# First block of a seven-product matmul with GELU: half of its contraction by eight plain products, taken as the tiles arrive

## The chip, the core and the metric

The kernel runs on one core of one Trainium2 chip. The metric is the device time of one execution in microseconds (us); lower is better. The kernel before takes 1603.82 us, the median of three runs that lie between 1603.33 and 1605.74 us. A separate profiled execution took 1601.1 us.

## The reference

```python
def reference(a, b):                      # a, b: 4096 x 4096, float32
    x = np.matmul(a, b)
    return 0.5 * x * (1 + np.tanh(np.sqrt(2 / np.pi) * (x + 0.044715 * x**3)))
```

One product of two 4096 x 4096 matrices, and the tanh form of GELU on each element of the result.

## The kernel before, in words

**Seven products for eight.** A, B and the output are cut into quadrants of 2048 x 2048, named "11", "12", "21", "22". A plain product of 2 x 2 quadrants needs eight quadrant products. This kernel makes seven, of sums and differences of quadrants (the list `PRODUCTS`), and puts the output together from running sums of them. The inputs are converted to fp16 on their way in and the products are summed in fp32.

**Groups.** The output is made in 16 groups (`groups`, four row blocks by four column blocks). A group makes one 512 x 512 piece of each of the four output quadrants. For it, each product has 512 rows, 512 columns and half of the contraction, 2048. A product is done in four steps (`QPH`, counted by `q`), each a contraction of 512. A step is 16 matmuls of 128x128 weights by 512 columns: four row tiles `i` times four pieces `j`. A group is therefore 7 x 4 x 16 = 448 matmuls, and the kernel 7168.

**Tiles.** A block of a quadrant is loaded in two chunks `c` of 1024 of the contraction, so steps q = 0, 1 of a product read chunk 0 and steps 2, 3 read chunk 1. A chunk is 1 MB in fp16, of A or of B. The first group needs 16 of them: four quadrants of A and four of B, two chunks each. `load_a` (L126 to L136) issues four DMAs of 256 KB into a `stage` tile, of which there are two (`bufs=2`). `turn_a` (L138 to L144) transposes the stage on the vector engine (DVE) into `aT`. `load_b` (L146 to L156) issues eight DMAs of 128 KB, each to 32 partitions, and its tiles need no transpose. All these loads are issued by GpSimd (POOL), in the order in which the program calls them.

**Sums.** `make_sums` (L248 to L260) makes the sum or difference that a step multiplies, for A (`aS`), for B (`bS`) or for both, on DVE (L256). It is called two steps ahead (`AHEAD = 2`, three buffers each). An operand that is a single quadrant is used as it was loaded.

**Banks and settling.** A group has two sets of four PSUM banks, X and Y, one bank for each row tile. Each of the seven products adds to X or to Y. When a product ends (`q == 3`), `settle` (L321 to L351) takes what is needed from the banks, one row tile at a time: copies by the scalar engine (ACT) in `keep` (L297), additions and subtractions on DVE in `tt` (L319), GELU by ACT in `emit` (L310) and the write of an output tile by a DMA that SyncE (SP) issues (L313). Output tiles rotate through four buffers `y`. After the product s = 3, for example, ACT copies X, and DVE makes two operations for each row tile.

**What sets the order.** The whole program is written out by hand (`manual_schedule`). For each step, the loop at its end (L442 to L451) first issues what `before` lists for it (loads, transposes, and in later groups squares that serve a range check of the inputs), then the sums for two steps later, then output tiles that wait, then the matmuls with their settling. Each engine works through its own list in that order. For the first group the loads and transposes are listed in one table (L361 to L374): first A11 chunk 0, B12 and B22 chunk 0, then chunk 1 of the same three, and so on. The first product is A11 times (B12 + B22), so the first matmul needs those three tiles. The next group's B tiles are loaded from the products s = 3, 4 and 6 on (L384 to L407), into slots that are free by then (`move_slots`).

Of the kernel before, what the change touches and what calls it, by code (L numbers as in the profile page):

```python
# [7 lines left out]
F32 = mybir.dt.float32  # L8
F16 = mybir.dt.float16
BF16 = mybir.dt.bfloat16  # L10
# [3 lines left out]
ALU = mybir.AluOpType  # L14
AX = mybir.AxisListType

P = 128
Q = 32
NC = 512
# [3 lines left out]
RT = 4  # L23
TM = RT * P
AHEAD = 2
# [12 lines left out]
]  # L38
NP = len(PRODUCTS)
QPH = 4  # L40


SQUARE_MAX = 2.0**26
# [45 lines left out]
def half_path(  # L89
# [9 lines left out]
    nc = tc.nc  # L99
    M, K = a.shape  # L100
    _, N = b.shape
# [5 lines left out]
    pool = ctx.enter_context(tc.tile_pool(name="sb", bufs=1))  # L107
    psum_pool = ctx.enter_context(tc.tile_pool(name="psum", bufs=1, space=bass.MemoryType.PSUM))
# [12 lines left out]
    a_tiles, b_tiles = {}, {}  # L121
    a_slot = {"11": 0, "12": 1, "22": 2, "21": 3}
    b_slot = {"12": 0, "22": 1, "21": 2, "11": 3}
# [34 lines left out]
    def part(tiles, blk, quad, q):  # L158

        t = tiles[blk, quad, q // 2].rearrange("p x y -> p (x y)")  # L160
        w = 4 * NC
        return t[:, (q % 2) * w : (q % 2 + 1) * w]

    energy, squares = {}, []
    W = 2 * NC
# [82 lines left out]
    def make_sums(mb, nb, s, q):  # L248
        _, oa, ob = PRODUCTS[s]
        got = []  # L250
        for tiles, blk, o, tag in ((a_tiles, mb, oa, "aS"), (b_tiles, nb, ob, "bS")):
            if isinstance(o, str):
                got.append(part(tiles, blk, o, q))
                continue
            t = pool.tile([P, 4 * NC], F16, name=tag, tag=tag, bufs=AHEAD + 1)
            nc.vector.tensor_tensor(  # L256
                out=t[:, :], in0=part(tiles, blk, o[0], q), in1=part(tiles, blk, o[1], q),
                op=ALU.add if o[2] > 0 else ALU.subtract,
            )
            got.append(t)  # L260
        sums[mb, nb, s, q] = got

    groups = []
# [5 lines left out]
    banks = {}  # L269
    post = {}  # L270

    def multiply(gi, s, q):
        mb, nb = groups[gi]
        chain = PRODUCTS[s][0]
        first = q == 0 and (s == 0 or s == 1)
        sa, sb = sums.pop((mb, nb, s, q))
        sa = sa.rearrange("p (jj m e) -> p jj m e", jj=2, e=2)
        sb = sb.rearrange("p (kt n) -> p kt n", n=NC)
        for i in range(RT):
            if first:  # L280
                par = (gi + (chain == "Y")) % 2
                banks[chain, i] = psum_pool.tile([P, NC], F32, name=f"acc{chain}", tag=f"bank{par}{i}")
            for j in range(4):
                nc.tensor.matmul(  # L284
                    banks[chain, i][:, :],
                    sa[:, j // 2, i * P : (i + 1) * P, j % 2],
                    sb[:, j, :],
                    start=first and j == 0,
                    stop=q == QPH - 1 and j == 3,
                    skip_group_check=True,  # L290
                )
            if q == QPH - 1:
                settle(gi, s, i)

    def keep(tag, src, bufs):
        t = pool.tile([P, NC], F32, name=tag, tag=tag, bufs=bufs)
        nc.scalar.copy(out=t[:, :], in_=src[:, :])  # L297
        return t
# [3 lines left out]
    def flush():  # L302

        for args in waiting:
            emit(*args)
        waiting.clear()

    def emit(gi, i, ih, jh, y, src):
        mb, nb = groups[gi]
        nc.scalar.activation(y[:, :], src[:, :], ACT.Gelu_apprx_tanh)  # L310
        r0 = ih * MH + mb * TM + i * P
        c0 = jh * NH + nb * NC
        nc.sync.dma_start(out=out[r0 : r0 + P, c0 : c0 + NC], in_=y[:, :])  # L313

    def new_y():
        return pool.tile([P, NC], F32, name="y", tag="y", bufs=4)

    def tt(o, x, y, op):
        nc.vector.tensor_tensor(out=o[:, :], in0=x[:, :], in1=y[:, :], op=op)  # L319

    def settle(gi, s, i):  # L321

        X, Y = banks.get(("X", i)), banks.get(("Y", i))
        if s == 1:
            m5 = keep("m5", X, 2)
            flush()
            y = new_y()
            tt(y, Y, m5, ALU.subtract)
            waiting.append((gi, i, 0, 1, y, y))
        elif s == 2:  # L330
            post["x7", i] = keep("x7", X, RT)
        elif s == 3:
            x1 = post["x1", i] = keep("x1", X, RT)
            x7 = post["x7", i]
            tt(x7, x1, x7, ALU.subtract)
            tt(x1, Y, x1, ALU.subtract)
        elif s == 4:
            y = new_y()
            emit(gi, i, 0, 0, y, X)
            x1 = post["x1", i]  # L340
            tt(x1, X, x1, ALU.add)
        elif s == 5:
            y = new_y()
            tt(y, post.pop(("x1", i)), Y, ALU.subtract)
            flush()
            waiting.append((gi, i, 1, 0, y, y))
        elif s == 6:
            y = new_y()
            tt(y, Y, post.pop(("x7", i)), ALU.add)
            flush()  # L350
            waiting.append((gi, i, 1, 1, y, y))  # L351


    before = {}

    def at(gi, s, q, fn, *args):
        before.setdefault((gi * NP + s) * QPH + q, []).append((fn, args))


    T0 = -3  # L360
    for step, quads in (  # L361
        (-3, ("A11 0", "B12 0", "B22 0", "T11 0", "A11 1", "B12 1", "B22 1")),
        (0, ("T11 1", "A12 0", "A12 1")),
        (2, ("T12 0", "A22 0", "B21 0")),
        (4, ("T12 1", "A22 1", "B21 1", "B11 0")),
        (6, ("T22 0", "B11 1", "A21 0")),
        (8, ("T22 1", "A21 1")),
        (18, ("T21 0",)),
        (20, ("T21 1",)),
    ):  # L370
        for what in quads:
            fn = {"A": load_a, "B": load_b, "T": turn_a}[what[0]]
            at(0, 0, step, fn, 0, what[1:3], int(what[4]))


    nxt_b = {"12": "22", "22": "21", "21": "12", "11": "11"}
# [7 lines left out]
    for gi in range(len(groups) - 1):  # L384
        (mb, nb), (mb1, nb1) = groups[gi], groups[gi + 1]
        na, nbb = mb1 != mb, nb1 != nb
        if na:
            at(gi, 3, 0, move_slots, a_slot, nxt_a)
        if nbb:
            at(gi, 3, 0, move_slots, b_slot, nxt_b)  # L390
        for c in range(CH):
            if nbb:
                at(gi, 3, 2 * c + 1, load_b, nb1, "12", c)
                at(gi, 4, 2 * c + 1, load_b, nb1, "22", c)
                at(gi, 6, 2 * c + 1, load_b, nb1, "21", c)
            if na:
                at(gi, 4, c, load_a, mb1, "11", c)
                at(gi, 5, 2 * c, turn_a, mb1, "11", c)
                at(gi, 5, 2 * c + 1, load_a, mb1, "12", c)
                at(gi, 6, 2 * c, turn_a, mb1, "12", c)  # L400
                at(gi, 6, 2 * c + 1, load_a, mb1, "22", c)
                at(gi + 1, 0, 2 * c + 1, turn_a, mb1, "22", c)
                at(gi + 1, 1, c, load_a, mb1, "21", c)
                at(gi + 1, 3 + c, 0, turn_a, mb1, "21", c)
            if nbb:
                at(gi, 6, 2 * c + 1, load_b, nb1, "11", c)


    for mb in range(NMB):
        for which, gi in (("b", mb * NNB + 1), ("a", mb * NNB + 2)):  # L410
# [4 lines left out]
            ]  # L415
            n_two = len(pieces) - NP * QPH + 2
            for x, piece in enumerate(pieces):
                n = max(x // 2, x - n_two)
                at(gi, n // QPH, n % QPH, square, which, blk, *piece)
                at(gi, (n + 1) // QPH, (n + 1) % QPH, add_squares)  # L420
            at(gi, 6, 2, weigh, which)
# [16 lines left out]
    at(len(groups) - 1, 4, 0, read)  # L438

    with tc.manual_schedule():  # L440
        steps = [(gi, s, q) for gi in range(len(groups)) for s in range(NP) for q in range(QPH)]
        for n in range(T0, len(steps)):  # L442
            for fn, args in before.get(n, ()):
                fn(*args)
            if 0 <= n + AHEAD < len(steps):
                gi, s, q = steps[n + AHEAD]
                make_sums(*groups[gi], s, q)
            flush()
            if n >= 0:
                multiply(*steps[n])  # L450
        flush()  # L451
    return said["value"]

# [1 line left out]
def kernel(tc: tile.TileContext, a: bass.AP, b: bass.AP, out: bass.AP):  # L455
    stands = half_path(tc, a, b, out)
    with tc.If(stands == 0):
        general_path(tc, a, b, out)
# [30 lines left out]
```

## Time and profile before

| | us |
|---|---|
| median of 3 runs | 1603.82 |
| profiled execution, its time | 1601.1 |
| profiled execution, its span | 1599.4 |
| TensorE (PE) busy with matmuls | 1554.7 |
| DVE busy | 1243.0 |
| ACT busy | 517.6 |
| POOL busy | 530.8 |

The span runs from the first to the last recorded instruction; the 1.7 us between it and the execution's time lie around it. Busy time is a sum over an engine's instructions. Since neighbouring matmuls overlap, their mean duration (L284, some 380 ns) is longer than the distance between two starts. The page also cuts the span into 40 slices of 40 us; a digit is a busy share in tenths, and PEclk is the clock that TensorE was granted, in tenths of full speed. "aS<-aT" means that the instruction writes the tile aS and reads the tile aT. In a list of groups the last column is the time for which the engine sat idle just before them, and what ended it.

### The profile page before, as it was taken

To read this page: it belongs to the slowest core of one execution; us is meant where nothing else is said; L and a number is where in the kernel's file an instruction comes from. 1 tells how busy PE (TensorE), PEld (TensorE's weight loads), DVE (VectorE), ACT (ScalarE), POOL (GpSimd) and SP (SyncE) were. 2 spreads that over 40 slices of the span, in tenths; PEclk is the share of its full clock that TensorE was granted. 3 is DMA by queue.
4 is the path that set the end of the run, shared out by engine and by line. 5 is a ranking of instruction groups with operands and counts; after the bars stand their busy time and mean duration, and the time that the engine had idled before them with its cause. 6 is when DMAs were issued, how large, how long until landed. Compare 5 with 4: busy or idle time off the path is not lost. (4 is left out here: it accounts for less than half of the span.)

```text
span 1599.4 us, 19504 instructions
## 1 busy us (share of the span) xinstructions
PE 1554.7 (97%) x7168; PEld 702.9 (44%) x7168; DVE 1243.0 (78%) x1368; ACT 517.6 (32%) x706; POOL 530.8 (33%) x964
## 2 busy tenths in 40 slices
PE   2899999999999999999999999999999999999998
PEld 1344444444444444444444444444444444444443
DVE  2777888867977788886778788887687778888774
ACT  0114446412111644532112354542111144464111
POOL 6554341440323244332123414345021443414300
PEclk9999999999999999999999999999999999999999
DMA  9998674790967688488296847778477885747802
GB/s 179 198 201 158 105 147 99 129 207 29 196 100 144 138 132 158 86 154 156 56 181 106 174 82 137 151 117 182 81 127 137 132 158 101 149 94 132 157 27 81
DMA packets 224791, 211.12 MB, mean 132 GB/s; under 512 B 19888, under 2 KB 191920, under 8 KB 224688
## 3 DMA queue, kind: packets, MB, share of 16 engines
q0 software_dynamic: 187392, 142.67, 61.1%
q1 hardware_dynamic: 37296, 67.13, 11.6%
q8 instruction: 58, 0.95, 0.2%
q14 instruction: 45, 0.37, 0.1%
HBM read 285.22 MB, written 67.11 MB: 220 GB/s over the span
## 5 line engine op out<-in xcount | busy, mean ns | idle before, releaser
L284 PEld LDWEIGHTS <-aS 128*128 128x128 f16 x5120 | 501.4, 98 | 614.5 <-issue 9.1
L152 POOL DMA_DIRECT2D bR<-in_b_dram x832 | 448.6, 544 | 720.2 <-DVE bS L256 357.8
L256 DVE TENSOR_TENSOR aS<-aT 128x2048 f16<-128x2048 f16 x320 | 388.1, 1219 | 157.8 <-PE accX L284 121.9
L284 PE MATMUL accX<-bS,aS 128*128 128x512 f16 x2048 | 446.9, 380 | 8.6 <-DVE bS L256 7.4
L256 DVE TENSOR_TENSOR bS<-bR 128x2048 f16<-128x2048 f16 x320 | 387.7, 1218 | 80.2 <-PE accX L284 43.5
L284 PEld LDWEIGHTS <-aT 128*128 128x128 f16 x2048 | 201.5, 98 | 274.5 <-issue 23.1
L284 PE MATMUL accY<-bS,aT 128*128 128x512 f16 x1024 | 228.5, 385 | 29.1 <-DVE bS L256 29.1
L310 ACT ACTIVATE y<-y 128x512 f32<-128x512 f32 x192 | 118.6, 630 | 343.6 <-DVE y L319 343.3
L284 PE MATMUL accX<-bS,aT 128*128 128x512 f16 x1024 | 223.9, 379 | 0.0
L284 PE MATMUL accX<-bR,aS 128*128 128x512 f16 x1024 | 223.6, 379 | 0.0
L284 PE MATMUL accY<-bR,aS 128*128 128x512 f16 x1024 | 223.6, 379 | 0.0
L284 PE MATMUL accY<-bS,aS 128*128 128x512 f16 x1024 | 223.6, 379 | 0.0
L319 DVE TENSOR_TENSOR energy<-energy,square 128x1024 bf16<-128x1024 bf16 x240 | 164.6, 686 | 10.1 <-ACT square L177 6.4
L132 POOL DMA_DIRECT2D stage<-in_a_dram x128 | 82.0, 646 | 251.9 <-DVE aT L143 235.7
L297 ACT COPY x<-accX 128x512 f32<-128x512 f32 x128 | 75.1, 587 | 238.3 <-PE accX L284 238.3
L177 ACT ACTIVATE square<-aT 128x1024 bf16<-128x1024 f16 x120 | 123.9, 1051 | 64.6 <-DVE energy L319 64.3
L177 ACT ACTIVATE square<-bR 128x1024 bf16<-128x1024 f16 x120 | 123.5, 1051 | 60.5 <-DVE energy L319 60.5
L297 ACT COPY m<-accX 128x512 f32<-128x512 f32 x64 | 37.1, 580 | 248.7 <-PE accX L284 248.7
L143 DVE STREAM_TRANSPOSE aT<-stage 128x2048 uint32<-128x2048 uint32 x32 | 73.8, 2306 | 27.0 <-DMA stage<-in_a_dram 26.9
L319 DVE TENSOR_TENSOR x<-accX,x 128x512 f32<-128x512 f32 x64 | 44.3, 692 | 43.0 <-ACT y L310 43.0
L310 ACT ACTIVATE y<-accX 128x512 f32<-128x512 f32 x64 | 38.2, 597 | 119.6 <-PE accX L284 119.6
L319 DVE TENSOR_TENSOR y<-accY,m 128x512 f32<-128x512 f32 x64 | 42.7, 687 | 14.2 <-ACT m L297 14.2
(24 smaller groups left out, 224.0 us busy)
## 6 DMA issues: line engine op xcount, KB each, us to landing
bR<-in_b_dram POOLq DMA_DIRECT2D x832, 128.0 KB, 5.3
out_dram<-y SPq DMA_DIRECT2D x256, 256.0 KB, 5.4
stage<-in_a_dram POOLq DMA_DIRECT2D x128, 256.0 KB, 7.0
row<-seen_d SPq DMA_DIRECT2D x2, 1.5 KB, 2.1
seen_d<-seen SPq DMA_DIRECT2D x1, 3.0 KB, 7.3
```

Source lines behind the costliest of these rows:

```text
L132: nc.gpsimd.dma_start(out=s[g * Q : (g + 1) * Q, :, :], in_=a_v[kh * CH + c, g, :, x0 : x0 + TM // Q, :],)
L143: nc.vector.transpose(dst, src)
L152: nc.gpsimd.dma_start(out=t[g * Q : (g + 1) * Q, e::2, :], in_=b_v[kh * CH + c, g, e, :, :, n0 : n0 + NC],)
L177: nc.scalar.activation(t[:, :], src, ACT.Square)
L256: nc.vector.tensor_tensor(out=t[:, :], in0=part(tiles, blk, o[0], q), in1=part(tiles, blk, o[1], q), op=ALU.add if o[2] > 0 else ALU.subtract,
L284: nc.tensor.matmul(banks[chain, i][:, :], sa[:, j // 2, i * P : (i + 1) * P, j % 2], sb[:, j, :], start=first and j == 0, stop=q == QPH - ...
L297: nc.scalar.copy(out=t[:, :], in_=src[:, :])
L310: nc.scalar.activation(y[:, :], src[:, :], ACT.Gelu_apprx_tanh)
L319: nc.vector.tensor_tensor(out=o[:, :], in0=x[:, :], in1=y[:, :], op=op)
```

## The change

Only the first group is computed in another way, and its loads are ordered anew; the arithmetic of the other 15 groups is as before.

- Chunk 0 of the first group (half of its contraction) is done as eight plain quadrant products (`PLAIN`), 16 steps of 16 matmuls. Chunk 1 is done by the seven products, with their steps q = 2 and 3 only, 14 steps. That makes 30 steps and 480 matmuls, where there were 28 and 448.
- The plain products need no sums. Their order, and that of the loads, is that in which tiles come in: A11 and B12 first, then B11, A12, B22, B21, A21, A22, all of chunk 0, and then chunk 1.
- The plain results of the output quadrants 11 and 22 stay in the banks X and Y, and the seven products add to them. Since X and Y also enter the other output quadrants later, corrections are kept: `c12`, one tile for each row tile, copied from the product "12" by ACT, to which DVE adds X and from which it subtracts Y; and `c21`, the product "21" copied by ACT. DVE adds them after the products s = 1 and s = 3, one more operation for each row tile.
- `warm` makes a tile of zeros on DVE and issues 28 matmuls with it ahead of everything else on PE. Their result is overwritten.
- The next group's B tiles of chunk 0 for "12" and "22" are issued one product earlier, since the first group no longer needs the slots.

The loads of B in 32 partitions (`load_b`) are the same in both kernels. The diff:

```diff
@@ -38,6 +38,14 @@
 ]
 NP = len(PRODUCTS)
 QPH = 4
+
+
+PLAIN = [
+    ("12", "11", "12"), ("11", "11", "11"), ("12", "12", "22"), ("11", "12", "21"),
+    ("21", "21", "11"), ("21", "22", "21"), ("22", "21", "12"), ("22", "22", "22"),
+]
+N_PLAIN = 2 * len(PLAIN)
+N_WARM = 28
 
 
 SQUARE_MAX = 2.0**26
@@ -269,26 +277,65 @@
     banks = {}
     post = {}
 
+    def bank(gi, chain, i):
+        par = (gi + (chain == "Y")) % 2
+        t = psum_pool.tile([P, NC], F32, name=f"acc{chain}", tag=f"bank{par}{i}")
+        banks[chain, i] = t
+        return t
+
+    def products(acc, sa, sb, i, start, stop):
+
+        sa = sa.rearrange("p (jj m e) -> p jj m e", jj=2, e=2)
+        sb = sb.rearrange("p (kt n) -> p kt n", n=NC)
+        for j in range(4):
+            nc.tensor.matmul(
+                acc[:, :], sa[:, j // 2, i * P : (i + 1) * P, j % 2], sb[:, j, :],
+                start=start and j == 0, stop=stop and j == 3, skip_group_check=True,
+            )
+
+    def warm():
+        z = pool.tile([P, NC], F16, name="zeros", tag="bS", bufs=AHEAD + 1)
+        nc.vector.memset(z[:, :], 0.0)
+        for i in range(RT):
+            bank(0, "X", i)
+            bank(0, "Y", i)
+        for _ in range(N_WARM):
+            nc.tensor.matmul(
+                banks["X", RT - 1][:, :], z[:, :P], z[:, :], start=True, stop=True, skip_group_check=True
+            )
+
+    def plain(n):
+
+        (quad, oa, ob), q = PLAIN[n // 2], n % 2
+        chain = "X" if quad == "11" else "Y"
+        seen = [x for x in range(len(PLAIN)) if PLAIN[x][0] == quad]
+        start = n == 2 * seen[0]
+        stop = n == 2 * seen[-1] + 1
+        for i in range(RT):
+            acc = banks[chain, i]
+            products(acc, part(a_tiles, 0, oa, q), part(b_tiles, 0, ob, q), i, start, stop)
+            if not stop:
+                continue
+            if quad == "12":
+                post["c12", i] = keep("x7", acc, RT)
+            elif quad == "11":
+                tt(post["c12", i], post["c12", i], acc, ALU.add)
+            elif quad == "21":
+                tag = ("energy1", "energy2", "square", "square")[i]
+                t = pool.tile([P, W], BF16, name="c21", tag=tag, bufs=1 + (i > 1)).bitcast(F32)
+                nc.scalar.copy(out=t[:, :], in_=acc[:, :])
+                post["c21", i] = t
+            else:
+                tt(post["c12", i], post["c12", i], acc, ALU.subtract)
+
     def multiply(gi, s, q):
         mb, nb = groups[gi]
         chain = PRODUCTS[s][0]
         first = q == 0 and (s == 0 or s == 1)
         sa, sb = sums.pop((mb, nb, s, q))
-        sa = sa.rearrange("p (jj m e) -> p jj m e", jj=2, e=2)
-        sb = sb.rearrange("p (kt n) -> p kt n", n=NC)
         for i in range(RT):
-            if first:
-                par = (gi + (chain == "Y")) % 2
-                banks[chain, i] = psum_pool.tile([P, NC], F32, name=f"acc{chain}", tag=f"bank{par}{i}")
-            for j in range(4):
-                nc.tensor.matmul(
-                    banks[chain, i][:, :],
-                    sa[:, j // 2, i * P : (i + 1) * P, j % 2],
-                    sb[:, j, :],
-                    start=first and j == 0,
-                    stop=q == QPH - 1 and j == 3,
-                    skip_group_check=True,
-                )
+            acc = bank(gi, chain, i) if first else banks[chain, i]
+            products(acc, sa, sb, i, first, q == QPH - 1)
             if q == QPH - 1:
                 settle(gi, s, i)
 
@@ -326,6 +373,8 @@
             flush()
             y = new_y()
             tt(y, Y, m5, ALU.subtract)
+            if gi == 0:
+                tt(y, y, post.pop(("c12", i)), ALU.add)
             waiting.append((gi, i, 0, 1, y, y))
         elif s == 2:
             post["x7", i] = keep("x7", X, RT)
@@ -334,6 +383,8 @@
             x7 = post["x7", i]
             tt(x7, x1, x7, ALU.subtract)
             tt(x1, Y, x1, ALU.subtract)
+            if gi == 0:
+                tt(x1, x1, post.pop(("c21", i)), ALU.add)
         elif s == 4:
             y = new_y()
             emit(gi, i, 0, 0, y, X)
@@ -351,26 +402,32 @@
             waiting.append((gi, i, 1, 1, y, y))
 
 
+    steps = [(0, -1, n) for n in range(N_PLAIN)]
+    steps += [(0, s, q) for s in range(NP) for q in range(QPH // 2, QPH)]
+    steps += [(gi, s, q) for gi in range(1, len(groups)) for s in range(NP) for q in range(QPH)]
+    position = {step: n for n, step in enumerate(steps)}
     before = {}
 
     def at(gi, s, q, fn, *args):
-        before.setdefault((gi * NP + s) * QPH + q, []).append((fn, args))
-
-
-    T0 = -3
-    for step, quads in (
-        (-3, ("A11 0", "B12 0", "B22 0", "T11 0", "A11 1", "B12 1", "B22 1")),
-        (0, ("T11 1", "A12 0", "A12 1")),
-        (2, ("T12 0", "A22 0", "B21 0")),
-        (4, ("T12 1", "A22 1", "B21 1", "B11 0")),
-        (6, ("T22 0", "B11 1", "A21 0")),
-        (8, ("T22 1", "A21 1")),
-        (18, ("T21 0",)),
-        (20, ("T21 1",)),
+        if gi == 0 and s >= 0:
+            q = max(q, QPH // 2)
+        before.setdefault(position[gi, s, q], []).append((fn, args))
+
+
+    for n, whats in (
+        (0, "A11_0 B12_0 T11_0 B11_0 A12_0"),
+        (2, "B22_0"),
+        (4, "T12_0 B21_0 A21_0 A22_0"),
+        (8, "T21_0 B12_1 B22_1 A11_1"),
+        (10, "T22_0 A12_1"),
+        (14, "T11_1 A22_1 B21_1 B11_1"),
+        (16, "T12_1 A21_1"),
+        (18, "T22_1"),
+        (24, "T21_1"),
     ):
-        for what in quads:
+        for what in whats.split():
             fn = {"A": load_a, "B": load_b, "T": turn_a}[what[0]]
-            at(0, 0, step, fn, 0, what[1:3], int(what[4]))
+            before.setdefault(n, []).append((fn, (0, what[1:3], int(what[4]))))
 
 
     nxt_b = {"12": "22", "22": "21", "21": "12", "11": "11"}
@@ -387,11 +444,12 @@
         if na:
             at(gi, 3, 0, move_slots, a_slot, nxt_a)
         if nbb:
-            at(gi, 3, 0, move_slots, b_slot, nxt_b)
+            at(gi, 3 - (gi == 0), 0, move_slots, b_slot, nxt_b)
         for c in range(CH):
             if nbb:
-                at(gi, 3, 2 * c + 1, load_b, nb1, "12", c)
-                at(gi, 4, 2 * c + 1, load_b, nb1, "22", c)
+                early = gi == 0 and c == 0
+                at(gi, 3 - early, 2 * c + 1, load_b, nb1, "12", c)
+                at(gi, 4 - early, 2 * c + 1, load_b, nb1, "22", c)
                 at(gi, 6, 2 * c + 1, load_b, nb1, "21", c)
             if na:
                 at(gi, 4, c, load_a, mb1, "11", c)
@@ -438,16 +496,19 @@
     at(len(groups) - 1, 4, 0, read)
 
     with tc.manual_schedule():
-        steps = [(gi, s, q) for gi in range(len(groups)) for s in range(NP) for q in range(QPH)]
-        for n in range(T0, len(steps)):
+        warm()
+        for n, step in enumerate(steps):
             for fn, args in before.get(n, ()):
                 fn(*args)
-            if 0 <= n + AHEAD < len(steps):
+            if n + AHEAD < len(steps):
                 gi, s, q = steps[n + AHEAD]
-                make_sums(*groups[gi], s, q)
+                if s >= 0:
+                    make_sums(*groups[gi], s, q)
             flush()
-            if n >= 0:
-                multiply(*steps[n])
+            if step[1] < 0:
+                plain(n)
+            else:
+                multiply(*step)
         flush()
     return said["value"]
 
```

## The prediction

> **What bounds the kernel now.** I read the strip of 40 slices first, then PE's waits, then PE and DVE in order of time over the first group.
>
> ```profile
> PE   2899999999999999999999999999999999999998
> ...
> DMA  9998674790967688488296847778477885747802
> ```
>
> PE is full from the fourth slice to the last. Only the first 120 us have room, and there DMA is full. The waits of PE in the first 140 us:
>
> ```profile
> PE accY L284 <- DVE bS L256: 29.1, 2, 22.6
> PE accX L284 <- DVE bS L256: 4.0, 1, 4.0
> PE accX L284 <- ACT m L297: 1.1, 1, 1.1
> ```
>
> That is 34.2 us of PE's 44.7 idle us (1599.4 less 1554.7). PE in order of time (start, length, what, idle before):
>
> ```profile
> 22.60 9.08 PE L284 MATMUL accY<-bS,aT 128*128 128x512 f16 x32 [22.60 <-DVE bS L256]
> 38.21 9.80 PE L284 MATMUL accY<-bS,aT 128*128 128x512 f16 x32 [6.53 <-DVE bS L256]
> ...
> 74.16 22.57 PE L284 MATMUL accX<-bS,aS 128*128 128x512 f16 x96 [4.00 <-DVE bS L256]
> ...
> 110.37 13.98 PE L284 MATMUL accY<-bR,aS 128*128 128x512 f16 x64
> 124.19 13.98 PE L284 MATMUL accY<-bS,aS 128*128 128x512 f16 x64
> ```
>
> 64 matmuls take 124.19 - 110.37 = 13.82 us, 0.2158 each, 3.45 a step. By the same view group 1 starts at 138.00. From there PE never waits until the last group, so what the change is worth is when group 1 starts. DVE shows why PE waited:
>
> ```profile
> 10.77 2.31 DVE L143 STREAM_TRANSPOSE aT<-stage 128x2048 uint32<-128x2048 uint32 x1 [10.77 <-DMA stage<-in_a_dram]
> 21.32 2.36 DVE L256 TENSOR_TENSOR bS<-bR 128x2048 f16<-128x2048 f16 x2 [8.24 <-DMA stage<-in_a_dram]
> 26.52 2.31 DVE L143 STREAM_TRANSPOSE aT<-stage 128x2048 uint32<-128x2048 uint32 x1 [2.84 <-DMA stage<-in_a_dram]
> 36.93 2.36 DVE L256 TENSOR_TENSOR bS<-bR 128x2048 f16<-128x2048 f16 x2 [8.10 <-DMA stage<-in_a_dram]
> 42.28 2.31 DVE L143 STREAM_TRANSPOSE aT<-stage 128x2048 uint32<-128x2048 uint32 x1 [2.98 <-DMA stage<-in_a_dram]
> ```
>
> Each line starts when a tile is in: the first at 10.77, the third at 21.32, the seventh at 42.28. (42.28 - 10.77) / 6 = 5.25 us a tile, so tile k is in at 5.5 + 5.25 k. PE starved for the third tile, then for the sixth.
>
> **What the Trainium skill says.** "TensorE: Matmul & The Clock Gate", section "Back-to-back issue gap", gives N/2.4 + 2.5 ns, 216 ns for 512 columns; the trace's 215.8 agrees. Its Part 1 on the HAM clock gate says that the clock halves after an idle window of about 3.4 us and returns after a busy one, and that the window runs freely. The trace agrees (window, PE busy, clock):
>
> ```profile
> 34.00:36.00 2.00, 0.00 (x0) 1.00 1.31 194
> 36.00:38.00 2.00, 0.00 (x0) 0.74 1.39 184
> 38.00:40.00 2.00, 1.79 (x5) 0.50 1.45 196
> ...
> 42.00:44.00 2.00, 2.00 (x7) 0.56 1.45 196
> 44.00:46.00 2.00, 2.00 (x11) 1.00 1.42 192
> ```
>
> The idle times of 6.53 and 4.00 us cost the clock, that of 1.13 did not. The price: 32 matmuls at full clock are 6.9 us; they took 9.08 and 9.80, so 2.2 and 2.9 us; the 96 took 22.57 less 0.16 of overlap against 20.7, so 1.7. The same Part 1 says that DVE and ACT take their work strictly in order; every stall below rests on that. "DMA: Bandwidth & Descriptors", section "SWDGE vs HWDGE vs iDMA", says that a DMA that converts types must be issued from GpSimd. All input is converted, and the page shows it on the one software queue: hence one order of arrival.
>
> **The change part by part.** I follow PE (us from the span's start).
>
> *Start.* The first step needs A11 and B12. Tile 2 is in at 5.5 + 10.5 = 16.0; A11 is transposed at 13.1. PE starts at 16.1, not 22.6.
>
> *Zeros.* A slow matmul is 0.43 us apart (weight loads start at 22.98, 23.41, 23.84), so 28 take 6.0 to 12.0 us and end by about 14, before 16.1: cost nothing. Their use is bounded too. With a slow clock four steps take 13.8 + 2.2 and end at 32.1; with a full one step 4 waits for B22, tile 5, in at 31.8. I take 2.1 lost by either way.
>
> *Plain steps 4 to 7* end at 32.1 + 13.8 = 45.9. B21, tile 6, is in at 37.0.
>
> *A new wait.* Step 8 needs A21 transposed. The tile is in at 42.3, but on DVE that transpose stands behind the four additions to c12, which wait for the end of step 7. The last ends at 45.9 + 0.7, the transpose at 48.9. PE stalls 3.1 us. Behind it on DVE are the transposes of A22 (48.9 to 51.3, wanted at 56) and A11's second chunk, nothing else.
>
> *Plain steps 8 to 15* end at 49.0 + 27.6 = 76.6. Copies of c12 and c21 on ACT take 0.59 each; a bank's next matmul is three row tiles, 2.6 us, later, so they are hidden, and so are the four subtractions on DVE (0.69). Uncovered, each four would cost PE about 0.7.
>
> *Loads.* POOL gains no DMA. The stages wait for transposes: tile 11 for 48.9, where POOL would come to it at about 54 (in the kernel before it issued tile 7 at 32.88, two tiles ahead). Tile 13 waits for 65.6, about 1 us late, with two B tiles behind it; the first is wanted by DVE at 85.5 and in at about 80. Tile 16 waits for 79.7 and is in at 90, wanted at 111. All hidden. The next group's four early tiles follow at 95 to 120, wanted at 126 and later. SP's list stays the same.
>
> *Seven products.* 14 steps, 48.3 us of PE. DVE has three transposes (7.0), 20 sums at 1.14 (22.8, pitch of neighbours, 60.53 to 61.67) and 32 settling operations at 0.66 (21.1; eight took 94.79 to 100.10): 50.9. So DVE, not PE, is the fuller engine here, as settling comes twice as often. Where it bites:
> - After s = 1 ACT loads its GELU table between copies, as before (1.13 there). I take 0.6.
> - s = 3 ends at 104.8. Its first copy is done at about 102.9; then 12 operations (8 before), each third waiting for the second, at 0.7 to 0.74, until 111.6; then the transpose of A21 (2.34) and one sum (1.22): 115.3. PE wants s = 5 at 111.6. Stall 3.7.
> - DVE then has one sum, four operations, four sums and the first output operation, 1.1 + 2.4 + 4.6 + 0.7, until 124.1. PE wants Y for s = 6 at 122.3. Stall 1.8; if the 3.7 cost the clock, its 1.7 takes this one's place.
>
> *Unknown.* A clock lost in the 3.1 us stall: 0 to 2.9. Output buffers: s = 5 and 6 now lie 6.9 us apart, and an output lands 5.4 us after issue, so DVE can wait for a buffer: 0 to 1.4 for PE. Together 0 to 4.3; I take 1.2, as 3.1 lies below both idle times that cost the clock.
>
> *Sum.* 16.1 + 480 x 0.2158 (103.6) + 2.1 + 3.1 + 0.6 + 3.7 + 1.8 + 1.2 = 132.2 for the start of group 1. The kernel before by the same sum: 22.6 + 96.7 + 11.7 + 6.8 = 137.8, where the trace has 138.0. So 5.8 us less: the start gains 6.5, 32 matmuls cost 6.9, waits and clock fall from 18.5 to 12.5, and rounding is the rest. The profiled 1601.1 becomes 1595.3; the median of the runs shown lies 2.7 above that execution, 1603.8 becomes 1598.0.
>
> **The rivals.**
> - *The clock falls in every stall* and the buffers make PE wait: 4.3 in place of 1.2, group 1 at 135.3, 1601.1. For it: 4.00 us sufficed; against: 3.1 is shorter than the window.
> - *DVE decides the second half* (slower). Place: from the first seven-product step at 76.6 to group 1. If each operation's end-to-start wait shows (32 x 0.09, 20 x 0.14), eight copies are waited for at the 0.57 seen at 64.66, and the clock falls in three stalls (5.1): 50.9 + 2.9 + 2.8 + 4.6 + 5.1 = 66, so group 1 at 142.6, 1608.4. It decides once this stretch passes 64.6 us (138.0 + 3.2 - 76.6). For it: DVE has more work than PE; against: neighbours overlap in the trace.
> - *Arrival still decides.* The transposed tiles of chunk 1 come 6 us later than reckoned, since their stages wait; all the gain goes: 1603.8. Against: 5 us of slack.
> - *More gain:* the 3.7 stall or its clock is absent: 1594.3.
> - The loads "by 32 partitions" are already in the kernel before: nothing.
>
> **Chances.** Forecast 0.50, 1598.0 (own range 1596 to 1600.3); clock 0.25; slower DVE 0.10; arrival 0.08; more gain 0.07. Counted as faster is a gain over 0.2% (3.2 us, about what a measurement can tell from no change). The clock rival lies at 2.7 and is split, 0.10 faster and 0.15 same. Faster 0.67, same 0.23, slower 0.10. The range 1595.5 to 1604.0 leaves out the slower case and ends of others, some 0.18.
>
> **What would show it.** PE's first real matmul near 16; a stall of about 3 us near 46 on the transpose of A21; no wait for DMA after 32; stalls on aS near 112 and on Y or the clock near 122; group 1 near 132. It is wrong if PE waits for tiles after 50, or if DVE's second half is longer than 58 us.

## The result and the profile after

The changed kernel takes 1596.83 us, the median of four runs (1594.52 to 1597.39), beside 1604.78 for the kernel before (four runs, 1603.33 to 1606.57). The ratio is 0.9947, with a 95% interval of 0.993 to 0.9964, which is 5.8 to 11.2 us less. The profiled execution took 1597.39 us with a span of 1595.7; that of the kernel before 1601.1 and 1599.4.

The waits of PE over the whole span (who waited for whom, us in total, times, longest):

```profile
PE accY L291 <- DMA bR<-in_b_dram: 6.6, 3, 6.1
PE accX L291 <- DVE bS L264: 4.1, 1, 4.1
PE accY L291 <- DVE aT L151: 3.1, 1, 3.1
PE accY L291 <- DVE aS L264: 3.0, 1, 3.0
PE accY L291 <- DVE y L366: 1.6, 1, 1.6
PE accX L303 <- DVE zeros L298: 1.3, 1, 1.3
PE accX L291 <- ACT m L344: 0.2, 1, 0.2
```

Where PE waited 29.1 + 4.0 us for sums of tiles that came late, it now waits 6.6 for tiles (besides the 7.9 that the zeros fill before the first tiles are in), and for three DVE steps that had no wait before: a transpose, a sum, and an operation that reads Y. The order in time says where:

```profile
1.31 7.93 PE L303 MATMUL accX<-zeros 128*128 128x512 f16 x28 [1.31 <-DVE zeros L298]
15.37 8.69 PE L291 MATMUL accY<-bR,aT 128*128 128x512 f16 x32 [6.12 <-DMA bR<-in_b_dram]
...
31.80 6.85 PE L291 MATMUL accY<-bR,aT 128*128 128x512 f16 x31 [0.25 <-DMA bR<-in_b_dram]
...
48.63 29.49 PE L291 MATMUL accY<-bR,aT 128*128 128x512 f16 x128 [3.08 <-DVE aT L151]
77.96 7.07 PE L291 MATMUL accY<-bS,aT 128*128 128x512 f16 x32
...
116.02 7.08 PE L291 MATMUL accY<-bR,aS 128*128 128x512 f16 x32 [3.00 <-DVE aS L264]
124.68 7.07 PE L291 MATMUL accY<-bS,aS 128*128 128x512 f16 x32 [1.58 <-DVE y L366]
131.58 13.98 PE L291 MATMUL accY<-bS,aT 128*128 128x512 f16 x64
```

Group 1 starts at 131.58, where it started at 138.00: 6.4 us earlier. DVE, before two of these waits:

```profile
45.67 0.69 DVE L366 TENSOR_TENSOR x<-x,accX 128x512 f32<-128x512 f32 x1 [0.18 <-PE accX L291]
46.27 4.50 DVE L151 STREAM_TRANSPOSE aT<-stage 128x2048 uint32<-128x2048 uint32 x2
...
104.17 0.69 DVE L366 TENSOR_TENSOR x<-x,x 128x512 f32<-128x512 f32 x1 [0.26 <-ACT x L344]
...
111.79 0.69 DVE L366 TENSOR_TENSOR x<-x,c 128x512 f32<-128x512 f32 x1
112.40 2.30 DVE L151 STREAM_TRANSPOSE aT<-stage 128x2048 uint32<-128x2048 uint32 x1
114.73 2.36 DVE L264 TENSOR_TENSOR aS<-aT 128x2048 f16<-128x2048 f16 x2
```

The two transposes (A21, A22) start at once after the last addition to c12, with no idle time before them. So no tile held them up; their place in the list did (e2 below tests it). At 104.17 begins the burst of 12 operations after s = 3, 8.2 us long; only behind it come the last transpose and the sum that PE needs for s = 5.

The 3.08 us also cost the clock. By windows (PE busy, clock, DMA share, GB/s):

```profile
46.00:48.00 2.00, 0.00 (x0) 1.00 1.29 202
48.00:50.00 2.00, 1.36 (x5) 0.80 1.23 201
50.00:52.00 2.00, 2.00 (x7) 0.50 1.24 204
52.00:54.00 2.00, 2.00 (x9) 0.85 1.23 201
```

128 matmuls took 29.49 less 0.16 of overlap, against 27.6 at full clock: 1.7 us. The 3.00 us at 116 cost nothing more: the 32 matmuls after it took 7.08.

The first group gained 6.4 us, yet the profiled executions differ by 3.7. The rest lies at the other end, where both kernels wait for the range check's numbers (`row`), which DVE needs before the sums:

```profile
1519.15 1.56 DVE L228 TENSOR_REDUCE v<-row 1x1 f32<-1x128 f32 x6 [3.39 <-DMA row<-seen_d]
```

PE at this place in the kernel before, and then in the changed one:

```profile
1530.10 20.88 PE L284 MATMUL accX<-bS,aS 128*128 128x512 f16 x96 [3.43 <-DVE bS L256]
```

```profile
1524.36 22.25 PE L291 MATMUL accX<-bS,aS 128*128 128x512 f16 x96 [4.10 <-DVE bS L264]
```

0.67 us more of wait and 1.37 of slow clock: 2.0 that the edit doesn't touch. The end of the span after the last product's start adds another 0.7 (21.63 for 20.96). This is chance of the execution: where the runs below leave this stretch as it is (e1, e2, e3, e5, e7), the same wait takes 3.42 to 4.45 us.

### The profile page after: what moved, and what is told of

It is laid out like the page before. It is cut to its first block, busy times and chain, and to the rows that moved or that the text cites. A ratio compares the mean times of both kernels' runs of the same rounds, so it can differ in the third digit from the quotient of the medians.

```text
span 1595.7 us, 19619 instructions
## 1 busy us (share of the span) xinstructions
PE 1568.2 (98%) x7228; PEld 708.3 (44%) x7228; DVE 1229.6 (77%) x1365; ACT 522.5 (33%) x714; POOL 530.9 (33%) x964
## 5 line engine op out<-in xcount | busy, mean ns | idle before, releaser
L291 PEld LDWEIGHTS <-aS 128*128 128x128 f16 x4960 | 485.6, 98 | 595.9 <-DVE aS L264 7.0
L264 DVE TENSOR_TENSOR aS<-aT 128x2048 f16<-128x2048 f16 x310 | 376.0, 1219 | 151.1 <-PE accX L291 117.4
L291 PE MATMUL accX<-bS,aS 128*128 128x512 f16 x1984 | 432.5, 380 | 4.3 <-DVE bS L264 4.1
L264 DVE TENSOR_TENSOR bS<-bR 128x2048 f16<-128x2048 f16 x310 | 375.5, 1218 | 52.5 <-PE accX L291 41.0
L291 PEld LDWEIGHTS <-aT 128*128 128x128 f16 x2240 | 219.6, 98 | 277.7 <-issue 12.4
L291 PE MATMUL accY<-bR,aS 128*128 128x512 f16 x992 | 216.7, 379 | 3.0 <-DVE aS L264 3.0
L291 PE MATMUL accY<-bS,aS 128*128 128x512 f16 x992 | 216.7, 379 | 1.6 <-DVE y L366 1.6
L291 PE MATMUL accX<-bS,aT 128*128 128x512 f16 x992 | 217.0, 379 | 0.0
L291 PE MATMUL accY<-bS,aT 128*128 128x512 f16 x992 | 216.7, 379 | 0.0
L185 ACT ACTIVATE square<-aT 128x1024 bf16<-128x1024 f16 x120 | 123.8, 1051 | 64.9 <-DVE energy L366 64.6
L291 PE MATMUL accY<-bR,aT 128*128 128x512 f16 x192 | 45.4, 398 | 9.7 <-DMA bR<-in_b_dram 6.6
```

The source lines that it names most:

```text
L185: nc.scalar.activation(t[:, :], src, ACT.Square)
L264: nc.vector.tensor_tensor(out=t[:, :], in0=part(tiles, blk, o[0], q), in1=part(tiles, blk, o[1], q), op=ALU.add if o[2] > 0 else ALU.subtract,
L291: nc.tensor.matmul(acc[:, :], sa[:, j // 2, i * P : (i + 1) * P, j % 2], sb[:, j, :], start=start and j == 0, stop=stop and j == 3, skip_g ...
```

## The experiments

My theory was that of the prediction: arrival sets the start, then the vector engine's order sets three waits, the clock adds to some of them, and the zeros do nothing. The rivals: that the zeros matter; that arrival takes over where a wait is taken away; that DVE is full, so that moving its work is useless. The plain products, the new order of the loads and the next group's early tiles were not tested apart from each other; that they give the gain together rests on the sums over the trace. In the first job (e1 to e4) the kernel before took 1605.27, in the second (e5 to e8) 1606.12. The intervals of single kernels are some 2.3 us either way, so that the lines of the profile decide as much as the medians; but a profile shows one execution only, and the first tiles and the price of a lost clock differ between executions.

**e1: no zeros.**

```diff
-N_WARM = 28
+N_WARM = 0
```

> The changed kernel without its 28 zero matmuls. My theory: they end at 9.2 us, the clock falls at about 12 before the data comes at 15.4, and step 4 waits for tile 5 at 31.5 anyway; so nothing is lost: 1596.8 us, within 0.8 of the changed kernel, group 1 still starting between 131 and 132.5. Rival (the zeros are part of the gain): the first steps come about 2 us later and so does group 1, some 1599.

Measured: 1597.0 us (1594.1 to 1598.32), ratio 0.9942 (0.9928 to 0.9956). Nothing lost, as expected. In the profile, though, group 1 started at 133.59, outside what I had given:

```profile
15.85 9.80 PE L291 MATMUL accY<-bR,aT 128*128 128x512 f16 x32 [15.85 <-DMA bR<-in_b_dram]
...
32.39 7.07 PE L291 MATMUL accY<-bR,aT 128*128 128x512 f16 x32
...
49.44 30.69 PE L291 MATMUL accY<-bR,aT 128*128 128x512 f16 x128 [3.07 <-DVE aT L151]
```

Step 6 starts 0.8 us later than with zeros (39.30 for 38.49): the first tiles were in half a microsecond later (15.85 for 15.37) and the first 32 matmuls took 9.80 for 8.69, but the waits for tile 5 fell away in return. The same stall at step 8 cost 2.9 us of clock here and 1.7 there, which makes up the 2.0 us at group 1. So the price of a lost clock moves between executions, and the zeros stay below what the medians can tell.

**e7: zeros up to the data.**

```diff
-N_WARM = 28
+N_WARM = 54
```

> The changed kernel with 54 zero matmuls in place of 28, so that PE is busy until about 15 us and the clock is full when the data comes. My theory: steps 0 to 3 run about 2 us faster, and step 4 then waits for tile 5, which is in at 31 to 31.8 as before: nothing gained, 1596 to 1597.5. Rival (the first product's slow clock is on the path): 2 us faster, 1594.8 or less, with step 4 starting before 30.5.

Measured: 1596.98 us (1594.82 to 1599.66), ratio 0.9945 (0.9931 to 0.9959). The first steps in its profile:

```profile
15.38 7.07 PE L291 MATMUL accY<-bR,aT 128*128 128x512 f16 x32
...
31.77 0.38 PE L291 MATMUL accY<-bR,aT 128*128 128x512 f16 x1 [2.42 <-DMA bR<-in_b_dram]
32.45 8.54 PE L291 MATMUL accY<-bR,aT 128*128 128x512 f16 x31 [0.30 <-DMA bR<-in_b_dram]
```

The first product now runs at full clock, and the 1.6 us that it saves turn up again in a wait of 2.42 us for tile 5. Nothing is gained, as expected; the rival needed step 4 before 30.5. What I had not expected: after that wait the clock fell, and 31 matmuls took 8.54 us where the changed kernel's took 6.85.

**e2: the transpose of A21 ahead of the additions.**

```diff
-        (8, "T21_0 B12_1 B22_1 A11_1"),
+        (7, "T21_0"),
+        (8, "B12_1 B22_1 A11_1"),
```

> The changed kernel with the transpose of A21 chunk 0 listed one step earlier, ahead of the additions to c12 on the vector engine. My theory: the stall of 3.08 us at step 8 goes, and with it the slow clock after it (1.7 us in the profiled execution); nothing else is late until the seven products, so group 1 starts 3.1 to 4.8 us earlier, near 127 to 128.5, and the time is 1592 to 1593.7. Rival (arrival decides next): the steps after 8 wait for the transpose of A22 or for tiles of chunk 1, and less than 1.5 us comes through, 1595.3 or more.

Measured: 1593.0 us (1591.52 to 1594.81), ratio 0.9925 (0.9911 to 0.994).

```profile
42.29 2.31 DVE L151 STREAM_TRANSPOSE aT<-stage 128x2048 uint32<-128x2048 uint32 x1 [13.93 <-DMA stage<-in_a_dram]
```

```profile
45.44 27.79 PE L291 MATMUL accY<-bR,aT 128*128 128x512 f16 x128
73.07 7.07 PE L291 MATMUL accY<-bS,aT 128*128 128x512 f16 x32
...
126.70 13.98 PE L291 MATMUL accY<-bS,aT 128*128 128x512 f16 x64
```

The transpose now starts when its tile is in, at 42.29. No wait at step 8, full clock after it, and group 1 is 4.9 us earlier, that is 3.1 + 1.7 and 0.1 from the steps before. Nothing waits for a tile after step 0. The rival that arrival comes next falls.

**e5: the stall filled, not shortened.**

```diff
+            if n == 8:
+                zeros(z, "Y", 14)
             if step[1] < 0:
                 plain(n)
```

> The changed kernel with 14 zero matmuls between steps 7 and 8, into a Y bank that is free then; they fill the stall before the transpose of A21 without shortening it. My theory: step 8 starts when it did, but the clock stays full, so the 1.7 to 2.9 us that the following 128 matmuls lost in the profiled executions are saved: they take 27.8 us in the profile, and the time is 1594 to 1595.5. Rival (the slow clock is not caused by the stall, or the zeros are in the way): within 0.7 us of 1596.8, or slower.

Measured: 1593.39 us (1592.27 to 1596.6), ratio 0.9932 (0.9918 to 0.9946).

```profile
44.70 3.19 PE L307 MATMUL accY<-zeros 128*128 128x512 f16 x14
47.94 27.80 PE L291 MATMUL accY<-bR,aT 128*128 128x512 f16 x128
...
113.63 8.54 PE L291 MATMUL accY<-bR,aS 128*128 128x512 f16 x32 [3.00 <-DVE aS L264]
122.29 7.07 PE L291 MATMUL accY<-bS,aS 128*128 128x512 f16 x32
```

The stall was there in full, yet the 128 matmuls kept the clock. That fits the theory that the idle time costs it, but this one profile does not show it: e3, below, kept the clock through the same stall without zeros (27.80 us after 3.07). The median fell by 3.4 us, more than the 1.3 to 2.8 that I expected. Of the 5.1 us between the two profiled executions the clock is 1.7; an earlier first tile is 0.7, and 2.7 lie in the last group, which the edit leaves alone. So what the zeros are worth here stays open. In this execution the 3.00 us at 113 did cost the clock (8.54 for 7.07), and the wait at s = 6 was gone in return. So these two do take each other's place.

**e3: c21 added later.**

```diff
-            if gi == 0:
-                tt(x1, x1, post.pop(("c21", i)), ALU.add)
...
             tt(y, post.pop(("x1", i)), Y, ALU.subtract)
             flush()
+            if gi == 0:
+                post["y", i] = y
+                for k in range(RT) if i == RT - 1 else ():
+                    y = post.pop(("y", k))
+                    tt(y, y, post.pop(("c21", k)), ALU.add)
+                    waiting.append((gi, k, 1, 0, y, y))
+                return
...
-        (24, "T21_1"),
+        (23, "T21_1"),
```

> The changed kernel with the four additions of c21 moved from the product s = 3 to after s = 5, behind the four operations that read Y, and the transpose of A21 chunk 1 one step earlier. The same number of vector operations in all. My theory: the vector engine's burst after s = 3 sets the start of s = 5, so the stall of 3.0 us there goes; the wait of 1.6 at s = 6 stays within 1 us; waits for output buffers at the start of group 1 take back 0 to 1.5: 1593.3 to 1595.3. Rival (the vector engine is full over the whole second half, so moving work changes nothing): the stall comes back at s = 6 or in group 1 in full, 1596.3 or more.

Measured: 1593.76 us (1591.96 to 1595.42), ratio 0.993 (0.9916 to 0.9944).

```profile
126.64 0.69 DVE L366 TENSOR_TENSOR y<-accY,x 128x512 f32<-128x512 f32 x1 [2.40 <-DMA out_dram<-y]
```

```profile
110.33 7.07 PE L291 MATMUL accY<-bR,aS 128*128 128x512 f16 x32
117.82 7.07 PE L291 MATMUL accY<-bS,aS 128*128 128x512 f16 x32 [0.43 <-DVE y L366]
124.73 7.07 PE L291 MATMUL accY<-bS,aT 128*128 128x512 f16 x32
132.66 7.07 PE L291 MATMUL accY<-bS,aT 128*128 128x512 f16 x32 [0.87 <-DVE bS L264]
```

The same vector work in another place: the wait at s = 5 is gone, that at s = 6 falls from 1.58 to 0.43, and 0.87 comes back in group 1, behind a wait of DVE for an output buffer (2.40 us). So DVE was not full over the stretch; a burst stood at the wrong place. The edit moves the additions and the last transpose together; what each of them gives was not measured.

**e4 and e8: the check's reads issued early, in the changed kernel and in the kernel before.**

```diff
-    at(len(groups) - 1, 2, 0, answer)
+    at(len(groups) - 1, 1, 2, answer)
```

> The changed kernel with the range check's two small reads issued one product's half earlier in the last group, so that they no longer stand behind output writes on the SyncE queue. Both kernels lose 3.4 to 4.1 us to this wait at about 1520 us, and where the clock falls after it another 1.4. My theory: this wait, with its clock, is what made the profiled difference (3.7 us) smaller than the first group's (6.4) and than the medians' (8): without it the changed kernel takes 1591.3 to 1593.4, and its runs lie closer together than the 2.9 us between them now. Rival (the wait is covered by something else that is late): within 1 us of 1596.8.

> The kernel before with the range check's two reads issued early as in the run with the early answer. My theory: that wait lies 1380 us behind the first group and is the same in both kernels, so it is worth the same here, 3.4 to 4.8 us: 1600.3 to 1602 where the kernel before has 1605.3. The gain of the change is then the same with this wait gone in both, 7.3 to 8.5 us. Rival (the changed kernel alone gains from it): within 1 us of the kernel before.

Measured: e4 1593.05 us (1589.27 to 1594.34), ratio 0.9921 (0.9906 to 0.9935); e8 1600.08 us (1597.14 to 1601.02), ratio 0.9967 (0.9954 to 0.998). In the changed kernel the two reads stand on SP behind four output writes that wait for their data; in e4 they come 20 us earlier:

```profile
1490.12 25.80 SPq L360 DMA_DIRECT2D out_dram<-y  x4
1516.02 1.86 SPq L222 DMA_DIRECT2D row<-seen_d  x2
```

```profile
1495.86 1.22 SPq L222 DMA_DIRECT2D row<-seen_d  x2
```

The product s = 2 of the last group in each, now without a wait:

```profile
1512.17 27.79 PE L291 MATMUL accX<-bS,aS 128*128 128x512 f16 x128
```

```profile
1518.68 27.79 PE L284 MATMUL accX<-bS,aS 128*128 128x512 f16 x128
```

e4 gains 3.8 us, as expected. Its runs do not lie closer together (5.1 us from lowest to highest), so this wait is not what spreads them; that part failed. e8 gains 6.0, more than the 4.8 that I had given. With the wait gone in both, the change is worth 1600.08 - 1593.05 = 7.0 us by the medians, and 6.5 by the start of group 1 in these two profiled executions (137.08 and 130.57). Both lie below the 7.3 to 8.5 that I had given.

**e6: the three edits of e2, e3 and e4 together.**

> The changed kernel with three edits together: the early transpose of A21, c21 added after s = 5 with the transpose of A21 chunk 1 one step earlier, and the early reads of the range check. My theory: the three waits lie apart and the gains add up (3.8, 3.1 and 3.8 by the medians): 1585 to 1587.5, with group 1 starting near 122 to 124. Rival (one engine or the arrival of tiles is next, and the gains overlap): 1589 or more.

Measured: 1583.21 us (1582.41 to 1584.18), ratio 0.986 (0.9845 to 0.9875). All waits of PE in its profile:

```profile
PE accY L291 <- DMA bR<-in_b_dram: 7.3, 2, 7.2
PE accX L303 <- DVE zeros L298: 1.3, 1, 1.3
PE accY L291 <- DVE y L366: 0.4, 1, 0.4
PE accX L291 <- ACT m L344: 0.3, 1, 0.3
PE accY L291 <- DVE aT L151: 0.3, 1, 0.3
```

This beats both kernels: 13.6 us below the changed one by the medians, more than the 10.7 that the single edits sum to and below what I had expected. The extra 3 us are no finding: 10.7 is a sum of three differences of medians, each of them uncertain by some 2 us and more. The profiled executions, 13.6 us apart too, account for it by place: group 1 starts at 124.32, 7.3 earlier; the wait in the last group and the clock after it, 4.1 + 1.4, are gone; the end of the span gives 0.7. After the first steps no wait is longer than 0.43 us and no stretch of the first or last group shows a lost clock, and its four runs lie within 1.8 us.

## Why the prediction was right

The sum gave 132.2 for the start of group 1; the trace has 131.58. Step by step:

- *Start*, 16.1 predicted: 15.37, and 14.3 to 16.0 in the runs of the experiments on the changed kernel. The reckoning of 5.25 us a tile held.
- *Zeros* cost nothing and bring nothing: they end at 9.2, e1 and e7 move the median by 0.2. The cap by tile 5 was reckoned at 31.8; step 4 waited for it at 31.2 and 31.8.
- *The new wait* at step 8, 3.1 predicted: 3.08, on the transpose behind the additions, as named.
- *Loads* hidden: PE waits for no tile after 32.
- *The burst* after s = 3, 3.7 predicted: 3.00, since the 12 operations took 8.2 us and not 8.7. *Y for s = 6*, 1.8 predicted: 1.58. *ACT's table*, 0.6 predicted: 0.20.
- *First steps*, 2.1 predicted for slow clock and tile 5: 2.4.
- *Unknown*, 1.2 taken for clock and buffers: the clock alone took 1.7 in the profiled execution. The buffers made DVE wait three times (1.20, 0.64, 0.64) and PE not at all. The reason that I gave, that 3.1 us lies below both idle times that cost the clock, was wrong; the wait of 3.43 in the last group, which I hadn't weighed, had cost none.
- *Luck.* That the sum came within 0.6 us is in part luck. Start and stalls came 2.1 us under the reckoning; first steps, clock, and some 0.16 us to get going again after each wait came 1.4 above it. In e1, whose edit is worth nothing by the medians, group 1 started at 133.59: 1.2 us of dearer clock, and 0.8 in the first steps. In e3 the stall at step 8 cost no clock at all.
- *Prices.* The 2.2 and 2.9 us for the first two lost clocks leave out the 0.16 of overlap that the third takes off, so they are a little high. And the 216 ns that I cited from the Trainium skill ("TensorE: Matmul & The Clock Gate", section "Back-to-back issue gap") is that section's figure for one matmul by itself; for a stream with weight loads it gives about 131 ns. The stream here runs at 215.8, so the measurement decides.
- *Size.* 5.8 us forecast, 8.0 measured, which has 5.8 at the near end of its interval. The first group gave 6.4 to 6.5: it started 7.2 us earlier, its 32 further matmuls took 6.9 of that back, and its waits and lost clock fell from 18.7 to 12.6. So most of the gain is that of the waits, as in the sum. The interval holds 6.5 as well as 8.0, and what is beyond 6.5 need not be the first group's: the profiled execution of the kernel before that I reckoned from, 1601.1, lies below every timed run of it (1602.23 and up), and taking the last wait away in both leaves 7.0. What still separates 7.0 and 6.5 is within the spread of the runs.

Of the rivals, that of the lost clock was half true in the profiled execution (first stall yes, second no), and the gain stayed. That of a DVE-bound second half was tested by e3 and fell: from 77.96 to 131.58 it took 53.6 us, far from the 64.6 at which it would have decided.

## What to carry to other kernels

Where arrival bounds a start, do the work that needs one tile of each operand first, even at the cost of more arithmetic, and check which tile the steps after it wait for: speeding up what stands ahead of that tile is worth nothing. Then read the strict lists of the helping engines: a transpose behind four additions that wait for the previous step costs a stall although its tile is there, and settling twice as often makes bursts; both were mended by moving lines in the list, not by doing less. Count every idle time of PE from about 2 us on, the shortest that cost the clock here, as a possible loss of clock besides, and remove it (e2); what filling it gives stays open (e5).

## What was not expected of the hardware

- Idle times of PE of nearly one length cost the clock or not, by execution. 3.07 to 3.08 us before the 128 matmuls cost 1.7 (changed kernel, e4), 2.9 (e1) or 1.5 (e7), and nothing in e3; 3.00 before s = 5 cost nothing in the changed kernel, 1.5 in e5 and 1.7 in e7; 3.43 in the last group cost nothing in the kernel before and 1.7 in e1. In e8 even the 2.10 us of the ACT table's wait cost 1.8 (24 matmuls took 7.17 less 0.16, for 5.18), while 2.49 us soon after it cost nothing:

```profile
65.26 7.17 PE L284 MATMUL accX<-bS,aS 128*128 128x512 f16 x24 [2.10 <-ACT m L297]
74.92 20.88 PE L284 MATMUL accX<-bS,aS 128*128 128x512 f16 x96 [2.49 <-DVE bS L256]
```

That it depends on the execution fits the freely running window that the Trainium skill describes ("TensorE: Matmul & The Clock Gate", Part 1 on the HAM clock gate). But by that page the clock falls after an idle window of about 3.4 us, and an idle time of 2.10 or 3.00 us cannot fill one. Here the measurement decides; how much of a window must be idle stays open.

- Matmuls with zeros count as work for the clock. In e7 six of them fall into the stretch from 2 to 4 us and eleven into that from 8 to 10, and the 32 matmuls after them take 7.07 us; without zeros (e1) these take 9.80. That they also hold the clock through a stall (e5) is not shown, since e3 held it without them.
- The clock column can mislead at the start: in e1 it reads 1.00 from 16 to 20 us, where five and six matmuls start in 2 us; at full clock it is eleven.
